# Hybrid encoder layer: where the embedding's products wait for their store, and the order of work in the state-space part

## The chip, the cores and the metric

The kernel runs on one core of one Trainium2 chip, in one launch. The metric is device time in microseconds. Of the kernel before, three runs took 2042.01 to 2043.56 us, median 2043.38 us. The profile is of one more execution.

## The reference, cut to what matters

One encoder layer on x (1024 tokens of width 1024, f32): a half-step feed-forward, one projection into attention and state-space inputs, attention and state-space side by side, an out-projection of both halves, a second half-step feed-forward, and an embedding gated into the result. Four layer norms stand between these.

```python
x = LN0(alpha*x + 0.5*SwiGLU_1(x))
u = x @ W_in                     # q | k | v | z | x_ssd | B | C | dt_fwd | dt_bwd
a = attention(q, k, v)           # 512 wide
s = ssd(x_ssd, B, C, dt)         # 512 wide: forward scan + backward scan + D * x, gated by SiLU(z)
x = LN1(alpha*x + concat(a, s) @ W_out)
x = LN2(alpha*x + 0.5*SwiGLU_2(x))
x = LN3(alpha*x + sigmoid(x @ W_g + b_g) * (p @ W_p))
```

The scan works on 8 chunks of 128 tokens; for one direction and one chunk it is

```python
y_diag = (C B^T * L) @ (x*dt)    # inside the chunk
y_off  = (C @ state) * decay     # what comes from the chunks before
state  = state * chunk_decay + B^T @ (x * dt * decay_to_end)
```

and the skip term adds `D * x`, one factor per head of 64 columns. Two places are touched by the change: `p @ W_p`, which does not depend on x and is computed at the very start, and the state-space scan with the out-projection around it.

## The kernel before, in words

Matrix products are made exact enough by splitting every f32 operand into a rounded high part and the rest (`split`, `split_into`, L79 to L87: ScalarE casts the high part, VectorE subtracts it for the low part), so a product of one 128-row step is three TensorE matmuls (`mm3`, L109). A block of weights that is split waits in the ring (tiles `blk`), what is not yet split in tiles `raw`. In parts of the program `in_order` fixes the order of an engine's instructions as the code is written; elsewhere a scheduler that plans ahead orders VectorE, ScalarE, GpSimd and the DMA queue of SyncE (SP's queue). TensorE's order is as the code is written throughout.

**The start** (`begin`, L561). While x is still being loaded, TensorE computes the embedding's product: 16 units (`ple_unit`, L577), each 128 tokens by 512 columns, 6 matmuls. A unit's result is copied out of PSUM into a small buffer (tiles `u2`, `u3`, `p5`, `p1`) by ScalarE, or for units 1, 3, 5 and 7 by VectorE, and stored in DRAM (`eD`); the store is issued by ScalarE (L590), behind its next copy. Between the units the list `beside` says which splits of x (`put`), differences (`less`) and splits of the first weights (`left`) are written there; TensorE, VectorE and ScalarE keep this order. x and the first weights come in by SP's queue. Two of the weights' blocks (`g0`, `u0`) are loaded into ring tiles behind the units. The products of the first feed-forward begin behind unit 15, so the third one of them (`p1`, L695) and all that follows waits for the 16 units.

**State space, right to left** (`ssd_right`, L1211). For the chunks 7 down to 0, three steps overlap: `front` (TensorE makes the decay exponents, ScalarE takes Exp of two 128x1024 tiles, and copies `cb`), `mid` (`y = D * x` by eight 128x64 ScalarE activations in `scale_heads`, then VectorE forms the weights `W`), `offdiag` with `next_state` (16 ScalarE activations, 128x64, and VectorE's adds), and `back` (8 small matmuls, the sum into `y`, a store to `yd`). At loop steps 0, 1 and 8 a filler is written behind: `spilled`, the attention half of the out-projection for one token tile, 24 matmuls of 128x512. Before the loop, `weights(0)` (L1479) splits that half's four weight blocks of 1024 columns, each as two halves in a row.

**State space, left to right** (`ssd_left`, L1282). For the chunks 0 up to 7: `offdiag`, `next_state`, the product with the gate `zs`, the norm, and a filler (five `resident`, out-projections that stay in memory, then five `mixed`, the state-space half of the out-projection with its layer norm). Two chunks later `turn` transposes the result on TensorE. The last `resident` calls `weights(1)`, which loads four 1024-wide blocks through the two `raw` tiles and splits them; the first `mixed` is the first to use them. Loads of the out-projection's accumulators (`acc1`, L1486, L1522), of the norm's factors (`ln_g`, `ln_b`), of `y2` (L1298), `zs`, `xb`, `bc` and of weights share SP's queue.

Of the kernel before, what the change touches and what calls it, by code (L numbers as in the profile page):

```python
# [9 lines left out]
F32 = mybir.dt.float32  # L10
# [26 lines left out]
class Layer:  # L37
# [522 lines left out]
    def begin(self, pool, tmp, spare):  # L560


        nc, I = self.nc, self.I
        V, A = nc.vector, nc.scalar
        self.eD = self.dram.tile([NT, P, D], F32, name="eD")
        a = slice(0, 512)

        first = [pool.tile([P, 4, 512], F32, name=f"xET4{j}") for j in "hl"]
        first = [t[:, k] for t in first for k in range(4)]
        todo, kept = [], []  # L570

        def loaded(src):
            r, b = first.pop(0), self.ring.tile([P, 2, 512], F32R, name="blk")
            nc.sync.dma_start(out=r, in_=src)
            todo.append((b, r))
            return b

        def ple_unit(i, t, n):
            c = slice((t % 4) * P, (t % 4 + 1) * P)
            o = self.pss()  # L580
            self.mm3(o, [((pT[t // 4][k][:, 0, c], pT[t // 4][k][:, 1, c]), (we[n][k][:, 0], we[n][k][:, 1])) for k in range(2)])
            e = tmp.tile([P, 512], F32, name=("u2", "u3", "p5", "p1", "p1", "p1")[i % 6])
            kept.append((self.eD[t][:, n * 512:(n + 1) * 512], e))
            if i < 8 and i % 2:
                V.tensor_copy(e, o)
            else:
                A.copy(out=e, in_=o)
                while kept:
                    dst, src = kept.pop(0)
                    A.dma_start(out=dst, in_=src)  # L590

        pT, we = [[], []], [[], []]

        def load_p(h, k):
            pT[h].append(loaded(I["pT"][:, k, h * 512:(h + 1) * 512]))

        def load_e(n, k):
            we[n].append(loaded(I["we"][n][:, k * 512:(k + 1) * 512]))

        for k in range(2):  # L600
            load_p(0, k)
            load_e(0, k)
        for load in (load_e, load_p):
            for k in range(2):
                load(1, k)
        nc.sync.dma_start(out=self.ident, in_=I["ident"])
        raws = []
        for k in range(4):
            for src in (I["xT"][:, k], I["xT"][:, k + 4]):
                i = len(raws)  # L610
                if i < 7:
                    r = self.rp.tile([P, D], F32, name="raw") if i < 5 else spare.tile([P, D], F32, name=f"wr{i - 4}")
                    nc.sync.dma_start(out=r, in_=src)
                    raws.append((r[:, :512], r[:, 512:]))
                else:
                    raws.append([tmp.tile([P, 512], F32, name=n) for n in ("h1", "h2")])
                    for j, r in enumerate(raws[-1]):
                        nc.sync.dma_start(out=r, in_=src[:, j * 512:(j + 1) * 512])
        sg = [tmp.tile([P, S], F32, name="sg") for f in range(3)]
        for f in range(2):  # L620
            nc.sync.dma_start(out=sg[f], in_=I["wi1"][f, 0])
        (r11, r12), (r21, r22) = ([[r[j] for r in raws[i::2]] for j in range(2)] for i in range(2))
        s = [tmp.tile([P, 512], F32, name=f"s{k + 1}") for k in range(4)]

        for b, r in todo:
            self.split_into(b, r)
        X = dict(zip(("B11", "B21", "T1", "B22"), sum(self.new_xT(), [])))
        for n in ("T2", "T3", "T4"):
            X[n] = [pool.tile([P, 4, 512], F32R, name=f"xE{n}{j}") for j in "hl"]

        def put(name, k, src):
            return lambda: self.put(X, name, k, a, src)

        def less(out, x, y):
            return lambda: V.tensor_tensor(out=out, in0=x, in1=y, op=ALU.subtract)

        w = {}

        def left(f, i):
            def do():  # L640
                w[f, i] = self.split(sg[f][:, i * 512:(i + 1) * 512])
            return do

        def sum1(k):
            return [less(r11[k], r12[k], r11[k]), less(s[k], r22[k], r11[k])]

        def staggered(first, then):

            return first(0) + sum((first(k + 1) + then(k) for k in range(3)), []) + then(3)

        def b11(k):
            return [put("B11", k, r11[k])]

        def b21(k):
            return [put("B21", k, r21[k])]

        def t2(k):
            return [put("T2", k, s[k])]

        def sum4(k):  # L660
            return [less(r21[k], r21[k], s[k])]


        beside = [[], b11(0) + b21(0), b11(1), b21(1) + sum1(0), b11(2), b21(2) + sum1(1), b11(3), sum1(2), b21(3), [left(0, 0)] + sum1(3),
                  [left(0, 1)] + t2(0) + sum4(0), [left(1, 0)] + sum4(1), [left(1, 1)] + t2(1) + sum4(2), t2(2) + sum4(3), t2(3), []]
        units = [(t, n) for u in range(2) for n in range(2) for t in range(u * 4, u * 4 + 4)]
        for i, ((t, n), work) in enumerate(zip(units, beside)):
            ple_unit(i, t, n)
            for do in work:
                do()  # L670
        work = []

        g0 = self.ring_raw(I["wi1"][0, 0])
        u0 = self.ring_raw(I["wi1"][0, 1])
        nc.sync.dma_start(out=sg[2], in_=I["wi1"][2, 0])
        a11, a12, a21, a22 = g0[:, :512], g0[:, 512:], u0[:, :512], u0[:, 512:]
        m = [tmp.tile([P, 512], F32, name=f"s{k + 1}") for k in range(4)]
        blocks0 = []

        def block(src):  # L680
            return lambda: blocks0.append(self.split(src))

        work += [lambda: V.tensor_tensor(out=m[0], in0=a21, in1=a22, op=ALU.add), less(m[1], m[0], a11), block(m[1]), block(m[0])]
        work += [put("T1", k, r11[k]) for k in range(4)] + [left(2, 0), left(2, 1), less(m[2], a11, a21)]
        work += staggered(lambda k: [less(r12[k], r22[k], r12[k])], lambda k: [put("T3", k, r12[k])])
        work += [block(m[2]), less(m[3], a12, m[1])]
        work += [put("T4", k, r21[k]) for k in range(4)]
        work += [block(a22), block(m[3])]
        work += [put("B22", k, r22[k]) for k in range(4)]
        pre = []  # L690
        for f, n in enumerate((5, 6, 7)):
            p1 = tmp.tile([P, 512], F32, name="p1")
            p = [self.product(w[f, i], X[b]) for i, b in enumerate(("B11", "B21"))]
            for _ in range(n):
                work.pop(0)()  # L695
            A.copy(out=p1, in_=p[0])
            V.tensor_tensor(out=sg[f][:, :512], in0=p1, in1=p[1], op=ALU.add)
            pre.append((p1, sg[f]))
        for do in work:
            do()  # L700
        return X, pre, blocks0
# [513 lines left out]
    def ssd_right(self, c, loaded, fillers):  # L1215
# [33 lines left out]

        def mid(ch, xb, bc, E, cb):  # L1250
            y = two.tile([P, 512], F32, name="y", bufs=3)
            self.scale_heads(y, xb, dsk)
            V.tensor_tensor(out=E[1], in0=E[1], in1=E[0], op=ALU.add)
            W = E[1]
            for g in range(2):
                V.tensor_tensor(out=W[:, 4 * g:4 * g + 4], in0=W[:, 4 * g:4 * g + 4], in1=cb[:, g].unsqueeze(1).broadcast_to([P, 4, P]), op=ALU.mult)
            return W, y
# [10 lines left out]
        for i in range(NT + 2):  # L1268
# [3 lines left out]
            if 0 <= ch + 1 < NT:  # L1272
                c1 = ch + 1
                xb, bc, E, cb = F.pop(c1)
                B[c1] = (c1, xb, bc) + mid(c1, xb, bc, E, cb)
                if st is not None:
                    self.offdiag(two, st, 1, c1, bc, B[c1][4])
                if c1 > 0:
# [6 lines left out]
    def ssd_left(self, c, loaded, late, mixT, fillers):  # L1285
# [28 lines left out]
        for ch in range(NT):  # L1314
# [3 lines left out]
            zs, y = rest.pop(ch)  # L1318
            if st is not None:
                self.offdiag(two, st, 0, ch, bc, y)  # L1320
            if ch < NT - 1:
                st = self.next_state(two, st, 0, ch, xb)
            V.tensor_tensor(out=y, in0=y, in1=zs, op=ALU.mult)
# [8 lines left out]
                o = slice(g * 256, (g + 1) * 256)  # L1332
                V.scalar_tensor_tensor(out=y[:, o], in0=y[:, o], scalar=r[:, g:g + 1], in1=snorm[:, o], op0=ALU.mult, op1=ALU.mult)
            waiting.append((ch, y))
            fillers[ch]()
            if len(waiting) > 2:
                turn(*waiting.pop(0))
        for w, filler in zip(waiting, fillers[NT:]):
            filler()
            turn(*w)  # L1340

# [74 lines left out]
    def run(self):  # L1416
# [61 lines left out]

        def weights(half):  # L1479
            if half:  # L1480
                wm[1].extend(self.wload(I["wm"][4 + k]) for k in range(4))
            else:
                wm[0].extend([self.split(r[:, i * 512:(i + 1) * 512]) for i in range(2)] for r in early)

        def attention_half(t, a):
            nc.sync.dma_start(out=a, in_=y0[t])  # L1486
# [253 lines left out]
```

## Time and profile before

| what | us |
|---|---|
| three runs, median (lowest, highest) | 2043.38 (2042.01, 2043.56) |
| profiled execution | 2044.08 |
| its span, first to last instruction | 2042.3 |
| TensorE busy | 1988.6 (97%) |
| VectorE busy | 1529.7 (75%) |
| ScalarE busy | 877.2 (43%) |
| GpSimd busy | 471.9 (23%) |

The profiled execution is 0.70 us above the median of the runs, and 1.8 us of it lie outside the span. TensorE is idle for 53.7 us of the span in all. In the rows, PE is TensorE, DVE is VectorE, ACT is ScalarE, POOL is GpSimd; SPq and ACTq are the DMA queues that SyncE and ScalarE feed. A timeline's row has the start, the time from there to the end of the group, and in brackets the idle time before it and what ended that.

### The profile page before, as it was taken

How to read it: one execution, taken by the hardware profiler on the slowest of the kernel's cores; microseconds unless marked ns; L12 is line 12 of the kernel's file. 1: busy time of each engine (PE TensorE's matmuls, PEld its weight loads, DVE VectorE, ACT ScalarE, POOL GpSimd, SP SyncE). 2: the span in 40 equal slices, each digit the busy share in tenths (PEclk: the TensorE clock that was granted, in tenths of full speed). 3: DMA queues.
4: the chain of work that ended last, by engine and by line, in shares of the span. 5: the costliest groups of instructions: out<-in, count | busy, mean ns of one | idle time of the engine just before them, and what ended most of it. 6: DMA issues, size and time to landing. Idle time of an engine off the chain costs nothing.

```text
span 2042.3 us, 25910 instructions
## 1 busy us (share of the span) xinstructions
PE 1988.6 (97%) x9244; PEld 1630.9 (80%) x9244; DVE 1529.7 (75%) x2289; ACT 877.2 (43%) x1552; POOL 471.9 (23%) x342
## 2 busy tenths in 40 slices
PE   8999999999999999999999999899999999999998
PEld 6788888887888889777887777678888888888886
DVE  6977876866669658658998769887777777567698
ACT  5433333324444124537888874333333333443311
POOL 0444445430001132000001001164444541000011
PEclk9999999999999999999999999999999999999999
DMA  7433553549865201230003382133444546986122
GB/s 259 150 119 139 191 185 139 186 171 345 283 233 176 79 29 57 62 115 11 1 1 114 100 299 83 67 128 133 178 174 152 190 142 241 366 271 226 50 73 93
DMA packets 145513, 306.80 MB, mean 150 GB/s; under 512 B 17218, under 2 KB 29890, under 8 KB 145384
## 3 DMA queue, kind: packets, MB, share of 16 engines
q1 hardware_dynamic: 143080, 300.96, 42.0%
q10 hardware_dynamic: 2304, 4.20, 0.5%
q8 instruction: 72, 1.18, 0.2%
q14 instruction: 57, 0.47, 0.1%
HBM read 213.67 MB, written 91.42 MB: 149 GB/s over the span
## 4 chain that ended last, share of the span: by engine, by line
PE 85%; DVE 6%; DMA 3%; ACT 2%; issue 2%; POOL 1%; SPq 0%; ACTq 0%; DVEq 0%; POOLq 0%
PE sm L117 49%; PE sm L482 12%; PE big L482 9%; PE big L117 3%; PE big L1053 3%; PE sm L1075 3%; PE sm L1090 1%; PE sm L1091 1%; DVE blk L85 1%; PE big L205 1%; DMA wr<-in_wo_dram 1%; PE sm L1159 1%; PE sm L1170 0%; DMA wr<-in_xT_dram 0%; DVE xl L85 0%
## 5 line engine op out<-in xcount | busy, mean ns | idle before, releaser
L117 PE MATMUL sm<-xh,blk 128*128 128x512 f32 x1424 | 448.4, 395 | 0.0
L117 PEld LDWEIGHTS sm<-xh,blk 128*128 128x128 f32 x1424 | 268.4, 189 | 62.7 <-DVE blk L85 0.3
L117 PE MATMUL sm<-xl,blk 128*128 128x512 f32 x736 | 288.3, 395 | 0.0
L117 PE MATMUL sm<-blk,xl 128*128 128x512 f32 (+2 forms) x784 | 240.6, 374 | 0.0
L117 PE MATMUL sm<-blk,xh 128*128 128x512 f32 (+2 forms) x584 | 207.2, 385 | 5.3 <-DVE blk L85 4.9
L103 ACT CAST blk<-raw 128x512 fp32r<-128x512 f32 (+1 forms) x166 | 99.6, 610 | 230.9 <-PE sm L117 145.1
L85 DVE TENSOR_TENSOR blk<-raw,blk 128x512 fp32r<-128x512 f32 (+1 forms) x166 | 162.3, 987 | 36.2 <-ACT blk L103 34.8
L85 DVE TENSOR_TENSOR blk<-s,blk 128x512 fp32r<-128x512 f32 x176 | 150.4, 859 | 40.1 <-ACT blk L103 38.2
L103 ACT CAST blk<-s 128x512 fp32r<-128x512 f32 x176 | 108.1, 621 | 158.3 <-PE sm L117 134.2
L180 POOL TENSOR_TENSOR ln_k<-ln_k,mhalf 128x1 f32<-128x1 f32 x32 | 41.1, 1290 | 561.1 <-DVE ln_k L179 544.1
L117 PEld LDWEIGHTS sm<-xl,blk 128*128 128x128 f32 x736 | 138.7, 189 | 32.7 <-DVE u L365 0.3
L117 PEld LDWEIGHTS sm<-blk,xl 128*128 128x128 f32 x784 | 143.3, 188 | 26.1 <-issue 0.7
L482 PE MATMUL sm<-xh 128*128 128x512 f32 x576 | 139.7, 391 | 1.9 <-DVE u L365 1.9
L85 DVE TENSOR_TENSOR xh<-blk,xh 128x1024 fp32r<-128x1024 f32 x78 | 96.8, 1241 | 57.0 <-ACT xh L430 50.9
L246 POOL TENSOR_TENSOR s<-raw 128x512 f32<-128x512 f32 x41 | 63.3, 1545 | 328.0 <-DVE blk L85 287.6
L117 PEld LDWEIGHTS sm<-blk,xh 128*128 128x128 f32 x584 | 110.3, 189 | 28.4 <-DVE blk L85 6.7
L85 DVE TENSOR_TENSOR xl<-blk,xl 128x1024 fp32r<-128x1024 f32 x76 | 92.8, 1220 | 49.6 <-ACT xl L430 45.0
L430 ACT CAST xl<-blk 128x1024 fp32r<-128x1024 f32 x76 | 79.8, 1050 | 115.2 <-PE big L482 39.8
L482 PEld LDWEIGHTS sm<-xh 128*128 128x128 f32 x576 | 107.7, 188 | 24.9 <-DVE u L365 2.3
L430 ACT CAST xh<-blk 128x1024 fp32r<-128x1024 f32 x78 | 81.9, 1050 | 103.7 <-PE sm L482 42.0
L482 PE MATMUL sm<-xl 128*128 128x512 f32 x480 | 117.0, 393 | 0.0
L117 PE MATMUL sm<-xET2h,blk 128*128 128x512 f32 x352 | 111.3, 397 | 1.2 <-DVE blk L85 1.2
(313 smaller groups left out, 4100.9 us busy)
## 6 DMA issues: line engine op xcount, KB each, us to landing
raw<-in_wi_dram SPq DMA_DIRECT2D x84, 512.0 KB
blk<-hS SPq DMA_DIRECT2D x154, 256.0 KB
hS<-h SPq DMA_DIRECT2D x88, 256.0 KB
wr<-in_wo_dram SPq DMA_DIRECT2D x44, 512.0 KB
blk<-wT SPq DMA_DIRECT2D x88, 256.0 KB
hS<-sg SPq DMA_DIRECT2D x66, 256.0 KB
wT<-wr SPq DMA_DIRECT2D x66, 256.0 KB
blk<-in_wo_dram SPq DMA_DIRECT2D x66, 256.0 KB
```

What stands on the lines that cost most here:

```text
L85: (eng or self.nc.vector).tensor_tensor(out=out, in0=full, in1=hi.bitcast(F32), op=ALU.subtract)
L103: self.nc.scalar.copy(out=b[:, 0, :n], in_=src)
L117: self.nc.tensor.matmul(ps, lhsT=a, rhs=b, start=(i == 0), stop=(i == n - 1))
L180: nc.gpsimd.tensor_tensor(out=r, in0=v, in1=self.mhalf[:, :1], op=ALU.pow)
L205: nc.tensor.transpose(out=ps[:, k], in_=a[:, k * P:(k + 1) * P], identity=self.ident)
L246: G.tensor_tensor(out=s1, in0=a21, in1=a22, op=ALU.add)
L430: A.copy(out=b[:, :, 0], in_=r)
L482: nc.tensor.matmul(ps[q], lhsT=b[:, 0, x, cut], rhs=b[:, 1, y], start=j == i == 0, stop=j == NP - 1 and i == 2)
L1053: nc.tensor.matmul(ps[:, n * 512:(n + 1) * 512], lhsT=Q[:, h, q0:q0 + P], rhs=K[:, h // 4, j, n * 512:(n + 1) * 512], start=j == 0, stop=j ...
L1075: nc.tensor.transpose(out=pt[:, k], in_=pr[:, kk * P:(kk + 1) * P], identity=self.ident)
L1090: nc.tensor.matmul(po, lhsT=vw, rhs=pth[:, k], start=k == 0, stop=False)
L1091: nc.tensor.matmul(po, lhsT=vw, rhs=ptl[:, k], start=False, stop=k == KD - 1)
```

## The change

At the start, all 16 units are copied out by ScalarE, four to a tile, into four tiles whose memory later holds blocks of x that are needed late (`xh10`, `xl10`, `xl11`, and `xET3h`); the 16 stores are issued on SP's queue, behind the loads of x and of the first weights. `g0` and `u0` become one tile `gu` in the memory of `xh11`, loaded ahead of the third `sg`. The splits in `beside` are spread anew: the `left` splits stand beside units 12 and 13 instead of 9 to 12. In the state-space part `y = D * x` becomes one VectorE multiplication per chunk; `weights(0)` and `weights(1)` split all first halves ahead of the second halves, and `weights(1)` loads 512-wide pieces. The filler of step 8 in `ssd_right` and the first one in `ssd_left` are written earlier: ahead of the last `offdiag` of the one and ahead of the first `next_state` of the other.

```diff
@@ begin
-            e = tmp.tile([P, 512], F32, name=("u2", "u3", "p5", "p1", "p1", "p1")[i % 6])
-            kept.append((self.eD[t][:, n * 512:(n + 1) * 512], e))
-            if i < 8 and i % 2:
-                V.tensor_copy(e, o)
-            else:
-                A.copy(out=e, in_=o)
-                while kept:
-                    dst, src = kept.pop(0)
-                    A.dma_start(out=dst, in_=src)
+            e = kept[i // 4][:, i % 4]
+            A.copy(out=e, in_=o)
+            with self.behind(mybir.EngineType.SP):
+                nc.sync.dma_start(out=self.eD[t][:, n * 512:(n + 1) * 512], in_=e)
...
-        for f in range(2):
-            nc.sync.dma_start(out=sg[f], in_=I["wi1"][f, 0])
+        gu = self.xp.tile([P, 4, 512], F32, name="xh11").rearrange("p (a b) c -> p a (b c)", b=2)
+        for dst, f, j in ((sg[0], 0, 0), (sg[1], 1, 0), (gu[:, 0], 0, 0), (gu[:, 1], 0, 1), (sg[2], 2, 0)):
+            nc.sync.dma_start(out=dst, in_=I["wi1"][f, j])
...
-        beside = [[], b11(0) + b21(0), b11(1), b21(1) + sum1(0), b11(2), b21(2) + sum1(1), b11(3), sum1(2), b21(3), [left(0, 0)] + sum1(3),
-                  [left(0, 1)] + t2(0) + sum4(0), [left(1, 0)] + sum4(1), [left(1, 1)] + t2(1) + sum4(2), t2(2) + sum4(3), t2(3), []]
+        beside = [[], b11(0) + b21(0), [], b11(1) + b21(1) + sum1(0), [], b11(2) + b21(2) + sum1(1), b11(3) + b21(3) + sum1(2), sum1(3),
+                  t2(0) + sum4(0), t2(1) + sum4(1), t2(2) + sum4(2), t2(3) + sum4(3), [left(0, 0), left(0, 1)], [left(1, 0), left(1, 1)], [], []]
...
-        g0 = self.ring_raw(I["wi1"][0, 0])
-        u0 = self.ring_raw(I["wi1"][0, 1])
-        nc.sync.dma_start(out=sg[2], in_=I["wi1"][2, 0])
-        a11, a12, a21, a22 = g0[:, :512], g0[:, 512:], u0[:, :512], u0[:, 512:]
+        X["T1"], X["T3"], X["T4"] = self.unit(1, 0), rest("T3"), rest("T4")
+
+        a11, a12, a21, a22 = (gu[:, i, j * 512:(j + 1) * 512] for i in range(2) for j in range(2))
@@ ssd_right
-            self.scale_heads(y, xb, dsk)
+            V.tensor_tensor(out=self.heads(y), in0=self.heads(xb[:, :512]), in1=self.per_head(dsk), op=ALU.mult)
...
                 B[c1] = (c1, xb, bc) + mid(c1, xb, bc, E, cb)
+                if c1 == 0:
+                    fillers.pop(i)()
                 if st is not None:
                     self.offdiag(two, st, 1, c1, bc, B[c1][4])
@@ ssd_left
                 self.offdiag(two, st, 0, ch, bc, y)
+            if ch == 0:
+                fillers.pop(0)()
             if ch < NT - 1:
                 st = self.next_state(two, st, 0, ch, xb)
...
-            fillers[ch]()
+            if ch:
+                fillers.pop(0)()
@@ weights
-                wm[1].extend(self.wload(I["wm"][4 + k]) for k in range(4))
+                blocks = []
+                for i in range(2):
+                    for k in (4, 6):
+                        r = self.rp.tile([P, 1024], F32, name="raw")
+                        halves = [r[:, j * 512:(j + 1) * 512] for j in range(2)]
+                        for j, h in enumerate(halves):
+                            nc.sync.dma_start(out=h, in_=I["wm"][k + j, :, i * 512:(i + 1) * 512])
+                        blocks += [self.split(h) for h in halves]
             else:
-                wm[0].extend([self.split(r[:, i * 512:(i + 1) * 512]) for i in range(2)] for r in early)
+                blocks = [self.split(r[:, i * 512:(i + 1) * 512]) for i in range(2) for r in early]
+            wm[half].extend(zip(blocks[:4], blocks[4:]))
```

The order of instructions moves at three places that matter. ScalarE at the start, behind the splits of p and of the embedding's weights; `raw` and `xh00`, `xh01` are x before and after the split, `sm` is PSUM. Before:

```order
L587 COPY u2_211<-sm_204 128x512
L590 DMA eD_127<-u2_211 128x512
L224 CAST xh00_190<-raw_147 128x512
L224 CAST xh01_192<-raw_149 128x512
L587 COPY p5_234<-sm_227 128x512
L590 DMA eD_127<-u3_221 128x512
L590 DMA eD_127<-p5_234 128x512
L224 CAST xh00_190<-raw_151 128x512
L224 CAST xh01_192<-raw_153 128x512
L587 COPY p1_260<-sm_253 128x512
L590 DMA eD_127<-p1_247 128x512
```

With the change:

```order
L585 COPY xh10_130<-sm_204 128x512
L585 COPY xh10_130<-sm_213 128x512
L224 CAST xh00_198<-raw_151 128x512
L224 CAST xh01_200<-raw_153 128x512
L585 COPY xh10_130<-sm_226 128x512
L585 COPY xh10_130<-sm_235 128x512
L224 CAST xh00_198<-raw_155 128x512
L224 CAST xh01_200<-raw_157 128x512
L585 COPY xl10_131<-sm_250 128x512
L585 COPY xl10_131<-sm_259 128x512
L224 CAST xh00_198<-raw_159 128x512
```

Units 0 to 5 now all end in a copy on ScalarE, where those of units 1, 3 and 5 were VectorE's, and the stores are gone from between its copies and casts.

SP's queue at the turn from the right part to the left part; `acc1` are accumulators of the out-projection, `y2` the chunks' sums that the left part goes on with. Before:

```order
L1486 DMA acc1_10327<-y0_86 128x1024
L1486 DMA acc1_10405<-y0_86 128x1024
L149 DMA ln_g_10280<-in_ln_g_dram 128x1024
L150 DMA ln_b_10281<-in_ln_b_dram 128x1024
L1298 DMA y2_10289<-yd_9562 128x512
L1298 DMA y2_10293<-yd_9562 128x512
L1298 DMA y2_10357<-yd_9562 128x512
L1298 DMA y2_10435<-yd_9562 128x512
L1486 DMA acc1_10483<-y0_86 128x1024
L1136 DMA xb_10520<-xbn_6914 128x768
```

With the change:

```order
L1507 DMA acc1_10228<-y0_86 128x1024
L1507 DMA acc1_10336<-y0_86 128x1024
L1507 DMA acc1_10414<-y0_86 128x1024
L1271 DMA yd_9549<-y_10134 128x512
L1507 DMA acc1_10503<-y0_86 128x1024
L1507 DMA acc1_10592<-y0_86 128x1024
L1543 DMA acc1_10717<-y1_9547 128x1024
L1543 DMA acc1_10819<-y1_9547 128x1024
L1543 DMA acc1_10891<-y1_9547 128x1024
L149 DMA ln_g_10211<-in_ln_g_dram 128x1024
L150 DMA ln_b_10212<-in_ln_b_dram 128x1024
L1307 DMA y2_10220<-yd_9549 128x512
```

Two accumulator loads of 512 KB stood ahead of the norm's factors and of the first `y2`; now eight do.

VectorE in the left part, around the norm of chunk 0 (`y2_10289` before, `y2_10220` with the change; `yss`, `rs_t` and `yr` are the norm's small tiles). Before, where `acc1_10405` is the second filler's accumulator:

```order
L1348 SCALAR_TENSOR_TENSOR acc1_10405<-sm_10407,acc1_10405 128x512
L1328 TENSOR_SCALAR yss_10312<-yss_10312 128x2
L124 TENSOR_TENSOR rs_t_10320<-yr_10318 128x2
L125 TENSOR_TENSOR rs_t_10320<-rs_t_10320,yss_10312 128x2
L126 TENSOR_SCALAR rs_t_10320<-rs_t_10320 128x2
L127 TENSOR_TENSOR yr_10318<-yr_10318,rs_t_10320 128x2
L1333 SCALAR_TENSOR_TENSOR y2_10289<-y2_10289,yr_10318,snorm_10287 128x256 x2
L1348 SCALAR_TENSOR_TENSOR acc1_10405<-sm_10421,acc1_10405 128x512
```

With the change, where `acc1_10414` is the third filler's:

```order
L1339 TENSOR_SCALAR yss_10273<-yss_10273 128x2
L1339 TENSOR_SCALAR yss_10321<-yss_10321 128x2
L1360 SCALAR_TENSOR_TENSOR acc1_10414<-sm_10430,acc1_10414 128x512
L124 TENSOR_TENSOR rs_t_10281<-yr_10279 128x2
L124 TENSOR_TENSOR rs_t_10329<-yr_10327 128x2
L125 TENSOR_TENSOR rs_t_10281<-rs_t_10281,yss_10273 128x2
L125 TENSOR_TENSOR rs_t_10329<-rs_t_10329,yss_10321 128x2
L126 TENSOR_SCALAR rs_t_10281<-rs_t_10281 128x2
L126 TENSOR_SCALAR rs_t_10329<-rs_t_10329 128x2
L127 TENSOR_TENSOR yr_10279<-yr_10279,rs_t_10281 128x2
L127 TENSOR_TENSOR yr_10327<-yr_10327,rs_t_10329 128x2
L1344 SCALAR_TENSOR_TENSOR y2_10220<-y2_10220,yr_10279,snorm_10218 128x256 x2
```

The last step of chunk 0's norm, on which its transposes wait, stood ahead of the second filler's last add, and now stands behind the third filler's.

## Rows read from the trace of the kernel before

**Rows 1.** The page, part 1: busy us, share of the span, instructions.

```profile
PE 1988.6 (97%) x9244; PEld 1630.9 (80%) x9244; DVE 1529.7 (75%) x2289; ACT 877.2 (43%) x1552; POOL 471.9 (23%) x342
```

**Rows 2.** Timeline of PE, first 45 us: start, us, instructions, idle before.

```profile
6.95 12.36 PE L117 MATMUL sm<-blk 128*128 128x512 f32 x42 [6.95 <-DVE blk L85]
22.33 14.16 PE L117 MATMUL sm<-blk 128*128 128x512 f32 x54 [3.02 <-DVE p L585]
36.33 0.40 PE L117 MATMUL sm<-xl,blk 128*128 128x512 f32 x1
...
37.02 0.39 PE L117 MATMUL sm<-xl,blk 128*128 128x512 f32 x1
```

**Rows 3.** Stretches: busy us (instructions) by engine, PEclk, DMA share, GB/s.

```profile
10.00:20.00 10.00, 9.31 (x36) 7.20 (x35) 3.37 (x5) 2.78 (x6) 0.00 (x0) 1.00 1.03 412
24.00:26.00 2.00, 2.00 (x6) 1.61 (x5) 2.00 (x5) 0.78 (x2) 0.00 (x0) 0.50 1.03 404
90.00:400.00 310.00, 309.94 (x1333) 250.75 (x1332) 233.50 (x293) 100.11 (x160) 145.56 (x97) 1.00 0.45 161
```

**Rows 4.** Timeline of ACT, 12 to 24 us.

```profile
18.61 0.33 ACTq L590 DMA_DIRECT2D eD<-u  x1
...
20.33 1.14 ACT L224 CAST xh<-raw 128x512 fp32r<-128x512 f32 x2 [5.35 <-DMA wr<-in_xT_dram]
```

**Rows 5.** Timeline of DVE, 12 to 32 us.

```profile
14.01 1.29 DVE L85 TENSOR_TENSOR xl<-raw,xh 128x512 fp32r<-128x512 f32 x2 [0.78 <-ACT xh L224]
```

**Rows 6.** Timeline of PE, 66 to 72 us.

```profile
68.75 0.73 PE L117 MATMUL sm<-xET2h,blk 128*128 128x512 f32 x2 [1.16 <-DVE blk L85]
```

**Rows 7.** What PE waited for, 1100 to 1178 us: us, times, longest.

```profile
PE sm L1159 <- DVE state L1176: 2.8, 4, 1.7
PE sm L117 <- DVE blk L85: 2.2, 3, 1.4
PE sm L1170 <- ACT xs L1153: 1.7, 2, 1.2
```

**Rows 8.** Stretches of the state-space part, columns as in rows 3.

```profile
1131.00:1163.00 32.00, 28.91 (x179) 22.55 (x178) 24.52 (x34) 32.00 (x113) 0.00 (x0) 1.00 0.37 111
1176.00:1178.00 2.00, 1.98 (x5) 1.14 (x6) 0.00 (x0) 2.00 (x9) 0.00 (x0) 0.58 0.50 178
1177.00:1199.00 22.00, 22.00 (x90) 17.94 (x91) 12.97 (x30) 16.15 (x66) 1.40 (x2) 0.94 0.98 370
...
1262.00:1280.00 18.00, 15.44 (x82) 12.61 (x83) 17.93 (x36) 12.09 (x28) 1.46 (x1) 1.00 0.22 89
```

**Rows 9.** Timeline of PE, 1100 to 1181 us: four chunks and the end.

```profile
1129.51 1.90 PE L1262 MATMUL sm<-xb,Eb 128*128 128x64 f32 x16
...
1135.14 1.89 PE L1262 MATMUL sm<-xb,Eb 128*128 128x64 f32 x16
...
1161.89 1.89 PE L1262 MATMUL sm<-xb,Eb 128*128 128x64 f32 x16
...
1176.02 2.17 PE L1170 MATMUL sm<-xs,xb 128*128 128x256 f32 x4 [1.20 <-ACT xs L1153]
1177.63 0.99 PE L117 MATMUL sm<-blk,xh 128*128 128x512 f32 x1
```

**Rows 10.** Timeline of SP's queue, 1170 to 1222 us.

```profile
1176.46 0.82 SPq L1486 DMA_DIRECT2D acc<-y  x2
...
1178.60 2.66 SPq L1298 DMA_DIRECT2D y<-yd  x4
```

**Rows 11.** Timeline of DVE, 1177 to 1200 us.

```profile
1186.72 0.69 DVE L1323 TENSOR_TENSOR y<-y,zs 128x512 f32<-128x512 f32 x1 [0.59 <-DMA y<-yd]
...
1191.61 0.88 DVE L1333 SCALAR_TENSOR_TENSOR y<-y,yr,snorm 128x256 f32<-128x256 f32 x2
```

**Rows 12.** What PE waited for, 1199 to 1346 us.

```profile
PE sm L117 <- DVE blk L85: 2.8, 1, 2.8
```

More of the change, by code (lines that the diff above doesn't have):

```diff
@@ L569, in begin @@
         first = [t[:, k] for t in first for k in range(4)]
-        todo, kept = [], []
+        todo = []
+        kept = [where.tile([P, 4, 512], F32, name=name) for where, name in ((self.xp, "xh10"), (self.xp, "xl10"), (pool, "xET3h"), (self.xp, "xl11"))]
         def loaded(src):
@@ L626, in begin, with rest @@
             self.split_into(b, r)
-        X = dict(zip(("B11", "B21", "T1", "B22"), sum(self.new_xT(), [])))
-        for n in ("T2", "T3", "T4"):
-            X[n] = [pool.tile([P, 4, 512], F32R, name=f"xE{n}{j}") for j in "hl"]
+        X = dict(B11=self.unit(0, 0), B21=self.unit(0, 1))
+        def rest(n):
+            return [pool.tile([P, 4, 512], F32R, name=f"xE{n}{j}") for j in "hl"]
+        X["T2"] = rest("T2")
         def put(name, k, src):
@@ L688, in begin, with b22, do @@
         work += [block(a22), block(m[3])]
-        work += [put("B22", k, r22[k]) for k in range(4)]
+        X["B22"] = None
+        def b22(k):
+            def do():
+                X["B22"] = X["B22"] or self.unit(1, 1)
+                self.put(X, "B22", k, a, r22[k])
+            return do
+        work += [b22(k) for k in range(4)]
         pre = []
@@ L1334, in ssd_left @@
             waiting.append((ch, y))
-            fillers[ch]()
+            if ch:
+                fillers.pop(0)()
             if len(waiting) > 2:
                 turn(*waiting.pop(0))
-        for w, filler in zip(waiting, fillers[NT:]):
+        for w, filler in zip(waiting, fillers):
             filler()
```

## The prediction

> **What bounds the kernel now.** I read the page's first part, then the timeline of TensorE, then the lists of what it waited for, and last the other engines' timelines where it waited. TensorE is busy for 1988.6 of 2042.3 us [rows 1]: the time is its work plus 53.7 us of idle time and of slow clock. Only what takes a TensorE wait away, or adds one, counts, and between the start and the state-space part such a shift passes on whole, since TensorE hardly waits there: 309.94 busy of 310 us [rows 3]. The diff touches two regions: the first 95 us, and 1097 to 1346 us (state space and out-projection).
>
> At the start TensorE gets its first split operands at 6.95 us, runs 42 of the 96 small products, waits 3.02 us for a VectorE copy, runs the other 54 and reaches the first feed-forward product at 36.33 us [rows 2]. Three matmuls take 0.70 us (36.33 to 37.02), 0.233 each, so the 54 should take 12.6 us; they took 14.0. The rest is the clock: the granted clock was 0.50 of the higher level, 2.4 GHz, in 24 to 26 us, after the wait [rows 3]. ScalarE is the cause of the wait: it had its store of `u` to issue and could not until 18.61, then `p` at 19.96, and between its copy and its casts of x at 20.33 it was idle 5.35 us [rows 4]. The transfers run at their limit meanwhile (412 GB/s, share 1.03) [rows 3].
>
> In the state-space part's right loop ScalarE is the bound: 32.00 of 32 us, TensorE 28.91, VectorE 24.52 [rows 8]. TensorE waits there for `state`, `xs` and the splits of the weights [rows 7]. In the left part the loads are at the limit first (share 0.98, 370 GB/s), and from about 1216 us VectorE: 17.93 of 18 us in 1262 to 1280, where TensorE has 15.44 [rows 8].
>
> **Start.** Removed: 16 store issues on ScalarE (0.33 us each, and the waits before them) and 4 copies on VectorE; added: 4 copies on ScalarE and 16 issues on SP's queue. The stores now go into memory that is not reused by the next unit, so no unit waits for a store. A copy takes 0.6 us against 1.4 us of a unit's six matmuls. If nothing else waits, TensorE runs all 96 in a row: 19.31 + 54 x 0.233 = 31.9 in place of 36.33, **-4.4**. What must then be ready at 31.9 are the splits of x's `B11` and the first weights, `left(0, 0)`, which wait for x (its last parts land about 20 us) and for some 28 VectorE operations at a pitch of 0.60 us (two in 1.29, each 0.69 long) [rows 5]: from the first of them at 14.01 that is 30.8, just hidden. If it isn't, each VectorE operation too late costs 0.6. On SP's queue the 16 stores (4 MB, about 10 us at 412 GB/s) stand ahead of the next weights, so those land by about 40 us, before the third product needs them. Given back: at 68.75 TensorE waits 1.16 us for a `blk` split [rows 6]; all before it is earlier, and with the change two more VectorE operations stand ahead of that split: **+0.7**, taken between 0 and 1.4. The start: **-3.7**, between -5 and -1 (only the 1.4 of clock gained).
>
> A rule speaks against this: the Trainium skill, "DMA: Bandwidth & Descriptors", section "Issuing engines are not separate DMA queues", says that transfers end up on the same 16 engines whoever starts them, and that another issuer only saves the sequencer's time. By it the move would save ScalarE's 16 x 0.33 us alone, none of it on TensorE's path, and the start would be 0. Here the row at 18.61 shows an issue that waits, with copies and casts behind it, so I hold with the row; the rule's case is a rival below.
>
> **Right part.** (1) `weights(0)` with first halves first: the first product needs 4 splits in place of 7. The three waits are 2.2 us [rows 7]; with splits at the pace of VectorE about 0.3 stays: **-1.9**. (2) `y = D * x`: 8 of the 27 ScalarE operations of a chunk go; one VectorE operation comes, 0.69 by the nearest row of its size, `y<-y,zs` [rows 11], taken between 0.6 and 1.2. By [rows 8], 113 ScalarE operations in 32 us are 4.2 chunks of 7.6 us, and 34 VectorE operations in 24.5 us, seven to a chunk, 5.0 us in each. ScalarE falls to under 6 us in a chunk, VectorE rises to 5.7, both about TensorE's own 5.63 (1129.51 to 1135.14) [rows 9]. Four chunks took 1161.89 - 1135.14 = 26.75 where 4 x 5.63 is 22.52: **-4.2**, of which up to 2 may stay if VectorE's turn comes late. (3) The filler moved ahead of the last `offdiag` covers the last `xs`: the wait of 1.20 goes, and with it the slow stretch behind it (granted clock 0.58 and 0.57 in four us, the first matmuls of 1176.02 and 1177.63 twice as long) [rows 8, 9], 1.7: **-2.9**. Sum **-9.0**: the first filler of the left part starts at about 1168.6, not 1177.63.
>
> **Left part.** (4) That filler now stands ahead of `next_state(0)`, so `offdiag(1)` follows `next_state(0)` with nothing between, and TensorE waits for the state's copy, 0.69 and the signals: **+0.9**. (5) SP's queue: 8 accumulators and 2 rows of factors, 5 MB, stand ahead of the first `y2`, where 2 MB did. Before, the four `y2` were issued from 1178.60 and the first was used at 1186.72 with 0.59 us of wait [rows 10, 11]. 3 MB more at 370 GB/s are 8.1 us; `y2` is there about 15 us behind the first filler's start, and the norm ends 5 to 6 us behind that (1186.72 to 1192.5 before). The transposes of chunk 0 come behind the third filler, about 22 us from the start: 5.6 (filler) + 0.9 + 0.9 + 1.7 + 5.6 + 1.7 + 5.6. So the load alone is just hidden, but VectorE now has the third filler's last add ahead of that norm's end: it can't go on before TensorE has ended the filler, and then takes 0.7 + 8 x 0.17 + 0.9 us and signals. TensorE waits 2.4 to 4.5 us where it didn't: **+3.7**. (6) `weights(1)` in halves: the wait of 2.8 us for its splits [rows 12] mostly goes, but VectorE is near its bound behind it, so I count half: **-1.4**, between 0 and -2.8. Left part **+3.2**, between 0 and +7.
>
> Sum: -3.7 - 9.0 + 3.2 = -9.5. The profiled execution of 2044.08 would be 2034.6; it stands 0.70 above the median of the runs, so about **2034 us**.
>
> **Rivals.** *The start gains nothing* (the rule above, as a mechanism of this kernel): the start is set by x's landing and by VectorE's 28 operations, and TensorE only waits at 31.9 instead of at 19.3. For it: transfers at their limit, VectorE 2.00 of 2 us in 24 to 26 [rows 3]. Against: VectorE loses four copies, and had only 3.37 of 10 us in 10 to 20, while ScalarE's casts came late. Then 2043.4 - 5.8 = 2037.6.
> *The left part takes the right part's gain back*: VectorE is the bound from 1216 to 1300, and its work there isn't less, so TensorE arrives 9 us earlier only to wait there. For it: 17.93 of 18 us. Against: before that stretch VectorE has 9 idle us in 1177 to 1199 (12.97 of 22) [rows 8], so its work can start earlier too. Right and left -1, start -1 to 0: 2041.5 to 2043, no change that can be told; 0.2%, 4.1 us, is about what a measurement of this kernel can tell.
> *Slower*: the eight accumulators hold SP's queue so long that `y2`, `xb` and the weights, all behind them, come late in turn. One accumulator is 512 KB, 1.4 us at 370 GB/s. It decides once the first `y2` lands later than 19 us behind the first filler, against my 15: then TensorE waits for each `turn` and `offdiag` of the left part, about 8 x 1.7 = 14 us beside the +3.2, and the gain of 12.7 becomes +4.5: 2048. For it: share 0.98 already. Against: the same bytes moved before, only in another order, and the loads start 9 us earlier.
>
> **How the numbers follow.** The forecast has 0.58, with its own range 2028 to 2038.5. The start without gain 0.18 (0.14 of it beyond 0.2%), the gain given back 0.17 (0.05 beyond), slower 0.07. So faster by over 0.2% has 0.77, within 0.2% 0.16, slower 0.07. The range for 8 in 10 goes from 2028 (start -5, right -9.7, left 0, the sum -14.7) to 2041, where the lower end of the given-back case lies.
>
> **What would show it.** Right: no TensorE gap between 19 and 23 us, the first feed-forward product near 32; in the right loop TensorE busy over 31 of 32 us and ScalarE below 30; the left part's first filler near 1165 (start included); a new wait of 2 to 5 us for `y2` or of about 0.9 us for `state` in the left part. Wrong: a wait for `blk`, `xl` or `raw` at 30 to 36 us; in the right loop a wait for `y`, `W` or `toff` on VectorE in place of `state`; more than two waits for `y2` in the left part; or the stretch 1216 to 1346 longer by what the right part gained.

## The result and the profile after

The changed kernel took 2026.26 us (median of 4 runs, 2023.06 to 2027.48), the kernel before beside it 2042.70: a ratio of 0.9921, interval 0.9903 to 0.9939. The forecast of 2034, range 2028 to 2041, had the direction; the time lies below the range. A second measurement, told below, gave 0.9931 (0.9919 to 0.9944), 2026.40 against 2040.42 from 21 runs of before.

The two profiled executions, cut where TensorE begins the same instruction in both:

| stretch | before | after | difference |
|---|---|---|---|
| start, to the first feed-forward product | 36.33 | 30.94 | -5.39 |
| from there to the right part (the change touches its first 60 us alone) | 1069.91 | 1064.56 | -5.35 |
| right part, to the left part's first filler | 71.39 | 61.33 | -10.06 |
| left part and out-projection | 131.23 | 132.83 | +1.60 |
| second feed-forward and the end | 733.44 | 733.74 | +0.30 |

0.87 us of the right part's 10.06 is `next_state(0)`, which now stands behind that filler: moved, not saved. So the right part gained 9.2, and the left part lost 0.7.

TensorE at the start of the changed kernel (start, us, instructions, idle before), to be held against [rows 2]; then its wait that answers to [rows 6]:

```profile
6.69 24.42 PE L117 MATMUL sm<-blk 128*128 128x512 f32 x96 [6.69 <-DVE blk L85]
30.94 0.40 PE L117 MATMUL sm<-xl,blk 128*128 128x512 f32 x1
...
63.88 0.73 PE L117 MATMUL sm<-xET2h,blk 128*128 128x512 f32 x2 [1.75 <-DVE blk L85]
```

The 96 products run in one piece. The wait at 64 us is 0.6 longer than before, but most of that is regained in the next 30 us: the twelfth product on `xET4l` starts 63.62 us behind the first feed-forward product, and in the kernel before 63.45. ScalarE in the same stretch, for [rows 4]: no store stands between copies and casts, and its idle times are those for TensorE's next result.

```profile
12.07 0.59 ACT L585 COPY xh<-sm 128x512 f32<-128x512 f32 x1 [0.94 <-PE sm L117]
12.55 1.14 ACT L224 CAST xh<-raw 128x512 fp32r<-128x512 f32 x2
13.60 0.59 ACT L585 COPY xh<-sm 128x512 f32<-128x512 f32 x1
14.82 0.59 ACT L585 COPY xh<-sm 128x512 f32<-128x512 f32 x1 [0.64 <-PE sm L117]
```

TensorE in the state-space part, for [rows 7, 9]: one wait at the entry, four chunks of 5.63 us, then the left part's new waits.

```profile
1100.81 0.50 PE L117 MATMUL sm<-blk,xh 128*128 128x512 f32 x1 [0.73 <-DVE blk L85]
...
1116.94 1.89 PE L1269 MATMUL sm<-xb,Eb 128*128 128x64 f32 x16
...
1139.46 1.90 PE L1269 MATMUL sm<-xb,Eb 128*128 128x64 f32 x16
...
1156.83 0.48 PE L117 MATMUL sm<-blk,xh 128*128 128x512 f32 x1
...
1164.31 1.13 PE L1166 MATMUL sm<-state,bc 128*128 128x256 f32 x4 [0.78 <-DVE state L1180]
...
1181.27 0.74 PE L1315 MATMUL sm<-ident,y 128*128 128x128 f32 x4 [2.06 <-DVE y L1344]
...
1228.38 0.83 PE L1315 MATMUL sm<-ident,y 128*128 128x128 f32 x4 [1.25 <-DVE y L1344]
```

Stretches of the changed kernel, columns as in rows 3, for [rows 8]. In the four chunks of the right loop all three engines are nearly full (first line), with TensorE setting the pace: ScalarE has 22.27 us of work in 22.52, 5.57 a chunk. Its 24.98 of 32 in the second line comes from the loop's end, where it has less to do. The clock falls behind the wait for `y2`; from 1196 to 1278 us VectorE is nearly full, 79.71 of 82 us.

```profile
1116.94:1139.46 22.52, 22.41 (x143) 18.29 (x144) 21.19 (x32) 22.27 (x74) 0.00 (x0) 1.00 0.51 154
1120.00:1152.00 32.00, 31.89 (x195) 26.45 (x196) 29.11 (x43) 24.98 (x76) 0.00 (x0) 1.00 0.37 116
1182.00:1184.00 2.00, 2.00 (x8) 1.59 (x7) 2.00 (x4) 0.58 (x1) 0.00 (x0) 0.58 0.95 335
1196.00:1207.00 11.00, 11.00 (x54) 9.11 (x53) 10.86 (x24) 8.60 (x30) 0.70 (x1) 1.00 0.70 229
1230.00:1243.00 13.00, 13.00 (x71) 10.97 (x70) 13.00 (x30) 6.59 (x17) 1.36 (x2) 1.00 0.30 121
1243.00:1261.00 18.00, 15.24 (x80) 12.15 (x78) 17.82 (x37) 12.70 (x28) 1.41 (x2) 1.00 0.15 59
```

### The profile page after: what moved, and what is told of

Same layout as the page of the kernel before. It is cut to its first block, busy times and chain, and to the rows that moved or that the text cites. A ratio compares the mean times of both kernels' runs of the same rounds, so it can differ in the third digit from the quotient of the medians.

```text
span 2023.4 us, 25860 instructions
## 1 busy us (share of the span) xinstructions
PE 1981.7 (98%) x9240; PEld 1628.7 (80%) x9244; DVE 1526.5 (75%) x2293; ACT 864.1 (43%) x1492; POOL 471.1 (23%) x342
## 4 chain that ended last, share of the span: by engine, by line
PE 89%; DVE 6%; issue 2%; DMA 1%; ACT 1%; POOL 1%; SPq 0%; DVEq 0%; POOLq 0%; ACTq 0%
PE sm L117 52%; PE sm L482 12%; PE big L482 9%; PE big L117 3%; PE big L1060 3%; PE sm L1082 3%; PE sm L1097 1%; PE sm L1098 1%; DVE blk L85 1%; PE big L205 1%; PE sm L1269 1%; PE sm L1177 1%; PE sm L1166 1%; DVE acc L191 0%; DMA raw<-in_wi_dram 0%
## 5 line engine op out<-in xcount | busy, mean ns | idle before, releaser
L85 DVE TENSOR_TENSOR blk<-s,blk 128x512 fp32r<-128x512 f32 x176 | 148.9, 851 | 37.9 <-ACT blk L103 36.1
```

Source lines behind the costliest of these rows:

```text
L85: (eng or self.nc.vector).tensor_tensor(out=out, in0=full, in1=hi.bitcast(F32), op=ALU.subtract)
```

## The experiments

Ratios are to the kernel before on the same chip, with their intervals. "Start" is the time of the first feed-forward product, "state space" the time from the right part's first decay exponents to the second feed-forward's first product (before: 36.33 and 202.6 us; changed: 30.94 and 194.2), both from each run's profile, which is one execution.

**The two halves of the change.** `start_only` is before with the hunks of `begin`, `scan_only` with all others.

> The kernel before with the change of the start alone (copies on ScalarE into late memory, stores on SP's queue, work beside the units spread anew); the state-space part is as before. The trace of the changed kernel gave 5.4 us in the start and 5.35 us in code that the change doesn't touch (3.3 at 468 to 502 us, 2.2 at 912 to 936 us). Theory 1: those 5.35 are differences between executions, so only the start counts: first feed-forward product near 31 us, 2037.5 us, and in the trace the wait at the L482 products near 470 may be there or not. Theory 2: they follow from the start: 2032 to 2034 us, and the trace has no TensorE wait over 0.5 us and no clock below 0.9 at 460 to 480 us.

> The kernel before with the state-space part's change alone; the start is as before. Theory 1: the difference of the two traces in that part holds: -10.1 in the right part, +1.6 in the left part, so -8.5: 2034 us; the first feed-forward product stays near 36.3 us. Rival: part of the 10.1 was only there because the part was entered with other DMA traffic or another clock: 2037 or more. If theory 2 of the run with the start alone holds, the wait near 472 us and the slow clock behind it are there as before.

`start_only` came to 0.9962 (0.9948 to 0.9976), start 30.36, state space 201.3; `scan_only` to 0.9962 (0.9949 to 0.9974), start 36.11, state space 195.2. The two add up to the whole, 0.9924. The median of `start_only`, 2032.71, lies where theory 2 had it, but both theories counted from the 2043 of the first runs; from the 2040.25 measured beside it, the 5.4 us of theory 1 are a ratio of 0.9974, within the interval. So the time alone does not decide. The stretch between the start and the state-space part does. It took 1069.9 in the profile of before, but 1064.8 with `scan_only`, whose start is that of before. Of all the kernels below, those with the old start took 1064.0 to 1067.8, those with the change's start 1064.6 to 1067.9. So its 5.35 us are a difference between executions (theory 1), and the profiled execution of before is a long one there. What varies is seen at the first down-projection products: TensorE in before, TensorE and then the stretch behind the wait in `y2_first` (told below), TensorE in the changed kernel:

```profile
472.01 1.98 PE L482 MATMUL sm<-xh 128*128 128x512 f32 x6 [1.88 <-DVE u L365]
```

```profile
466.56 1.65 PE L482 MATMUL sm<-xh 128*128 128x512 f32 x6 [1.97 <-DVE u L365]
```

```profile
468.00:472.00 4.00, 4.00 (x12) 3.10 (x12) 4.00 (x6) 1.31 (x2) 0.00 (x0) 0.57 0.98 348
```

```profile
465.12 1.66 PE L482 MATMUL sm<-xh 128*128 128x512 f32 x6 [0.24 <-DVE u L365]
```

The wait for `u` is 1.9 us long in the first two, with the clock near its lower level behind it, and this place takes 3.3 us more there than in the third, where it is 0.24. The long one comes with either start; over all fourteen profiles it lies between 0.24 and 1.97.

**What in the start did it.** `act_stores` is the changed kernel with the stores back on ScalarE, `dve_copies` with four copies back on VectorE, `small_tiles` with the small buffers back:

```diff
-            with self.behind(mybir.EngineType.SP):
-                nc.sync.dma_start(out=self.eD[t][:, n * 512:(n + 1) * 512], in_=e)
+            A.dma_start(out=self.eD[t][:, n * 512:(n + 1) * 512], in_=e)      # act_stores
...
-            A.copy(out=e, in_=o)
+            V.tensor_copy(e, o) if i < 8 and i % 2 else A.copy(out=e, in_=o)  # dve_copies
...
-            e = kept[i // 4][:, i % 4]
+            e = tmp.tile([P, 512], F32, name=("u2", "u3", "p5", "p1", "p1", "p1")[i % 6])  # small_tiles
```

> The changed kernel with the 16 stores of the embedding's products issued by ScalarE, each right behind its copy, in place of SP's queue; the memory that they are stored from is that of the change. My theory: what cost time was a store that had to wait, with copies and casts behind it on ScalarE; with ScalarE as issuer each issue takes 0.33 us and waits for the DMA eight before it, so part of the gap comes back: first product at 33 to 36 us, 2 to 5 us slower than the change (2028 to 2031). Rival, the memory alone did it (no reuse, so no wait): the first product stays at 31 to 32 us and the time within 1 us of the change's 2026.

> The changed kernel with the results of units 1, 3, 5 and 7 copied by VectorE as before, still into late memory and stored from SP's queue. My theory: the copy on VectorE, in order behind subtractions that wait for x, was where TensorE's 3.02 us wait ended; it comes back in part, first product at 33 to 35 us, 2 to 4 us slower than the change. Rival, the stores' issue on ScalarE alone was the cause: first product at 31 us, the same time as the change.

> The changed kernel with the 16 copies made into the small buffers of before (reused within the start), while the stores stay on SP's queue behind the loads. Theory: memory and queue belong together: the seventh copy waits for the first store, which stands behind 6.5 MB of loads until about 28 us, so the first feed-forward product comes at 42 us or later, 11 us or more slower than the change. Rival: the queue alone did it and the stores land in time: first product at 31 to 33 us.

`act_stores`: 0.9972 (0.9961 to 0.9983), start 37.33, more than my bounds: all of the start's gain is gone. `dve_copies`: 0.9942 (0.9929 to 0.9956), start 30.82: VectorE's copies cost the start nothing, my theory falls. `small_tiles`: one run, 2036.53; start 38.38, where I expected 42 or later. Memory and queue are both needed. ScalarE in `act_stores`, then in `small_tiles`:

```profile
13.27 0.59 ACT L585 COPY xh<-sm 128x512 f32<-128x512 f32 x1 [2.08 <-DMA raw<-in_xT_dram]
18.50 0.33 ACTq L586 DMA_DIRECT2D eD<-xh  x1
18.87 1.14 ACT L224 CAST xh<-raw 128x512 fp32r<-128x512 f32 x2 [5.01 <-DMA wr<-in_xT_dram]
```

```profile
27.70 0.59 ACT L585 COPY u<-sm 128x512 f32<-128x512 f32 x1 [8.31 <-DMA eD<-u]
```

The copy at 13.27 is done by 13.9, yet its store goes out at 18.50, when a load of x has landed: the issue waits for an earlier transfer of another queue, with casts and copies behind it. This wait is one of the program. In the trace the DMAs of both queues count their landing on eight semaphores in turn, and each issue first waits for the DMA eight before it, which had the same one. ScalarE has an instruction for that ahead of every store:

```profile
L586 ACTq EVENT_SEMAPHORE  x16: 17/17/17, 12.8 to 40.7; - x16
```

The store of 18.50 counts on the semaphore that the load of `wr` issued at 9.37 had last; in the kernel before it is the same for the store at 18.61 [rows 4]. So the rival of a start that gains nothing falls. By the rule of the Trainium skill behind it ("DMA: Bandwidth & Descriptors", section "Issuing engines are not separate DMA queues") another issuer saves only the time to issue. Here the first product comes 6.4 us later with ScalarE as issuer, and what holds ScalarE up is not the issue, 0.33 us, but the wait ahead of it, 5.01 us. Stores on ScalarE with semaphores of their own were not run. In the row of `small_tiles` the copy waits for the store of its buffer, which stands behind the loads.

**The parts of the state-space change.** Before with one part each (the hunks of the front's diff): `y_only`, `fillers_only`, `weights_only`.

> The kernel before with D * x on VectorE alone. Theory: in the right loop the four waits for state (2.8 us) and the wait for xs inside the loop (0.5) go, chunks take 5.63 us each, and ScalarE's xs at the end comes earlier, so that the wait of 1.20 us before the last next_state goes too: 4 to 7 us, 2034 to 2036. Rival: VectorE is now late in the loop, so waits for state stay and half or less is gained.

> The kernel before with the two fillers moved alone. Theory: the wait of 1.20 us for xs and the slow clock behind it go (2.9 us), the right loop keeps its waits for state, and the left part gets its new waits of 0.8 for state and 2 us for y2 with a slow clock behind: 0 to 1.5 us less than the kernel before. Rival: the wait for xs only moves, since ScalarE is behind in the loop: slower by 1 to 3 us.

> The kernel before with the order of the out-projection's weight splits alone. Theory: 1.8 us less at the entry of the right part (its waits of 2.2 us fall to about 0.7), and the wait of 2.8 us before the state-space half's first product goes, but VectorE, the bound behind it, takes that back: 1.8 us less in all. Rival: both stay, 4 us less.

`y_only` 0.9981 (0.9971 to 0.9991), state space 201.1, less than the 4 to 7 us expected: the waits for `state` are gone, that for `xs` (1.20) is not; 4.6 us are gained up to the first transposes and 3.1 given back behind them (its profiled execution is the longest of its ten). `fillers_only` 0.9990 (0.9981 to 1.0000), 201.3, close to what was expected, with new waits of 0.78 and 2.33 us. `weights_only` 1.0008 (0.9994 to 1.0021), 207.8: a miss. Its entry gains 1.8 us, and then TensorE waits the longer for ScalarE, which stays the bound, and runs near the lower clock behind that. (The profiled execution, 2046.38, is one of three among ten that took 2046 to 2049; the median is 2040.78, so 207.8 is more than usual, and what the usual execution does with the 1.8 us was not seen.) Its right loop and the stretch after:

```profile
1117.00:1161.00 44.00, 37.91 (x224) 28.44 (x222) 32.23 (x45) 44.00 (x152) 0.00 (x0) 1.00 0.33 106
1160.00:1172.00 12.00, 10.78 (x35) 9.25 (x36) 4.32 (x7) 2.00 (x9) 0.00 (x0) 0.57 0.19 66
```

Alone the three come to 0.9979, together to 0.9962. With the intervals of the three taken together (0.9960 to 0.9998) that difference is not shown. What the traces show is that the earlier entry is lost where ScalarE holds the loop back, and that the wait for `xs` of 1.20 goes with a filler in its place and stays without one.

**The left part.** `y2_first` is the changed kernel with the loads of six accumulators behind those of `y2`; `both` also cuts the first filler in two; `gate_pool` is `both` with the gate's product on GpSimd:

```diff
-            nc.sync.dma_start(out=a, in_=y0[t])
+            if t < 5:
+                nc.sync.dma_start(out=a, in_=y0[t])
+            else:
+                with self.tc.issue_after(self.y2_load):       # the y1 loads of mixed likewise
+                    nc.sync.dma_start(out=a, in_=y0[t])
...
-            fillers = [lambda t=t: resident(t) for t in range(3, NT)] + [lambda t=t: mixed(t) for t in range(3)]
+            fillers = [lambda n=n: half3(n) for n in range(2)] + [lambda t=t: resident(t) for t in range(4, NT)] + [lambda t=t: mixed(t) for t in range(3)]  # both; half3(n): half n of tile 3's filler
...
-            V.tensor_tensor(out=y, in0=y, in1=zs, op=ALU.mult)
+            nc.gpsimd.tensor_tensor(out=y, in0=y, in1=zs, op=ALU.mult)   # gate_pool
```

> The changed kernel with the accumulators of tiles 5 to 7 and 0 to 2 loaded behind the y2 loads, alone. Theory: the wait of 2.06 us for y2 at the first transposes and the slow clock behind it go, the 0.78 us for state stays: 3.7 us less than the change. Rival: the loads are late anyway, the wait for y2 stays above 1.5 us; or it turns into a wait for an accumulator that is now late, at the third filler (near 1176 us).

> The changed kernel with two more edits in the left part: the accumulators of tiles 5 to 7 and 0 to 2 are loaded behind the y2 loads on SP's queue, and the first filler is cut in its two halves of 12 matmuls, one ahead of next_state(0), one behind it. Theory (the left part's new waits come from the queue's order and from the missing cover): the waits of 0.78 us for state and 2.06 us for y2 go, and with the second the slow clock behind it (0.58 and 0.57 in four us), 1.7 us: 4.5 us less than the change, ratio to the kernel before near 0.990, 2020 to 2023 us. Rival (VectorE bounds the part from about 1200 us on): TensorE only waits later, first transpose near 1177 us but the out-projection's end within 1 us of the change's, and the time is the change's.

> The kernel with both edits of the left part, and in addition the gate's product y2 * zs of the eight chunks (128x512) on GpSimd in place of VectorE. Theory (what those two edits freed was taken back because VectorE is the bound from 1196 to 1278 us, 80.7 of 82 us busy): 8 operations of 0.6 us less on VectorE give 3 to 5 us between the first transpose and the out-projection's end against the run of both edits; ratio to the kernel before near 0.992. Rival: a GpSimd operation of this size takes about 1.3 us, lies in the chain of each chunk's norm, and the transposes wait for it: no gain.

`y2_first` 0.9946 (0.9931 to 0.9961), state space 194.6; `both` 0.9947 (0.9935 to 0.9960), 195.3: no gain in either, as the rival of `both` had it. TensorE in `both`:

```profile
1183.87 0.50 PE L117 MATMUL sm<-blk,xh 128*128 128x512 f32 x1 [1.01 <-DVE acc L1360]
...
1235.36 0.83 PE L1316 MATMUL sm<-ident,y 128*128 128x128 f32 x4 [1.82 <-DVE y L1345]
...
1265.96 1.12 PE L232 MATMUL big<-ident,xt 128*128 128x128 f32 x4 [4.68 <-DVE xt L1609]
...
1288.82 0.66 PE L232 MATMUL big<-ident,xt 128*128 128x128 f32 x4 [3.11 <-DVE xt L1609]
```

The first transposes wait no more, and TensorE is 3.3 us earlier there; but it waits longer for VectorE behind (4.68 where the change has 1.74 and 2.29), and the end is no earlier. `gate_pool`: 0.9923 (0.9910 to 0.9937), median 2024.76, state space 191.3, 4.1 less than `both` though each product takes 1.27 us or more on GpSimd: that fits VectorE's work as the bound (the expectation's 80.7 of 82 us is 79.71 in the trace of the change). Against the changed kernel's 2026.40, measured beside it, the gain is 1.6 us, and the intervals overlap: the best median, not shown to be faster than the change.

One rival stands. The scheduler orders VectorE anew in every kernel, and the second `xt`, for which TensorE waits 4.68 us in `both`, comes behind six splits of the next feed-forward's weights (`blk`) there, behind four in the changed kernel and behind one in `gate_pool`. VectorE in `both`, then in `gate_pool`:

```profile
1263.42 1.28 DVE L85 TENSOR_TENSOR blk<-sg,blk 128x512 fp32r<-128x512 f32 x2
...
1265.22 0.68 DVE L1609 TENSOR_TENSOR xt<-acc,acc 128x512 f32<-128x512 f32 x1
```

```profile
1257.98 0.69 DVE L85 TENSOR_TENSOR blk<-blk 128x512 fp32r<-128x512 f32 x1
1258.58 0.69 DVE L1609 TENSOR_TENSOR xt<-acc,acc 128x512 f32<-128x512 f32 x1
```

Five splits at a pitch of 0.6 us are 3 us, most of what lies between the two kernels. Whether VectorE's work or this order takes the gain of `both` back was not separated.

**The size again.** 

> The changed kernel once more, beside the kernel before on one chip. Its first runs gave a ratio of 0.9921 (0.9903 to 0.9939) from four runs of each; the terms that the two traces show in code that the change touches (start -5.4 and +0.6, right part -10.1, left part +1.6) are -13.3 us, a ratio of 0.9935, and kernels that differ from the change by little gave 0.9942 to 0.9947. If those terms are the whole effect, the ratio is 0.993 to 0.995. Rival: the 5.35 us in code that the change doesn't touch belong to it: 0.991 or less.

0.9931 (0.9919 to 0.9944), start 31.64, state space 193.0: the touched code's terms are the whole effect, as far as the interval tells.

## Why the prediction was wrong

The mechanisms were there; the sizes were too small, and the base was high. From 2034 to 2026.3 there are 7.7 us:

- **The base, 3.0.** I set the change against the median of three runs, 2043.38. In 21 runs the kernel before had 2040.42 (2036.57 to 2043.49); the three were among its longer ones, and my range carried nothing for that. With forecast and range 3.0 us lower the time would lie inside the range. I also counted on 0.2%, 4.1 us, as a difference that can be told; three runs of a kernel whose runs spread over 7 us don't give that.
- **Start, -3.7 forecast, -5.7 found.** First product: five kernels with the old start have 36.1 to 38.1, mean 36.8; seven with the change's start (`dve_copies` among them) 30.4 to 31.6, mean 30.8: -5.9, where I had -4.4. Of this, 0.5 is the trace of before, which lies on the short side: the five have gaps of 2.45 to 3.94 us with 3.5 to 6.0 us at the slow clock behind them, the trace of before 3.02 and 3.8. The rest is my 31.9: I counted from the end of the 42nd product at 19.31, while in the changed kernel the 43rd starts at 18.70, and the 54 take 12.24 us in place of 12.6. Given back: the wait at 64 us grew by 0.6 (forecast 0.7), but 0.2 is left of it by 100 us. The cause was right in the stores' issue on ScalarE; the copies on VectorE, taken away with it, had no share.
- **Right part, -9.0 forecast, -9.2 found.** Entry 1.8 (1.9); four chunks 1139.46 - 1116.94 = 22.52 (22.52 forecast); the rest is the filler over `xs`. Right, and VectorE was no bound, at 5.30 us in a chunk (5.7 forecast) beside TensorE's 5.63. ScalarE's 7.6 us in a chunk of before came of counting 27 operations to a chunk; ScalarE is full in the four chunks, so it is 26.75 / 4 = 6.7 us. It entered no term as a number.
- **Left part, +3.2 forecast, +0.7 found.** The wait for `state` came as worked out, 0.78 (0.9 forecast). That for `y2` was 2.06, under the 2.4 to 4.5 that I had; 1.7 of slow clock behind it, which I hadn't counted, bring it to the 3.7 forecast, by luck. The step that failed is to add the two to the time, with nothing given back behind them. TensorE then waits less for VectorE: the wait of 2.8 for `weights(1)` went whole where I counted half (in `start_only`, whose state-space part is that of before, it is 0.90, so part of it is the one trace), the layer norms' waits fell from 9.1 to 7.2 us, and one of 1.25 came. From 1196 to 1278 us VectorE is busy 79.71 of 82 us, and `both` takes the two waits away and ends no earlier. My second rival had the bound right and the consequence wrong: VectorE swallowed not the gain of the right part but most of the loss of the left. Whether through its work or through its planned order stays open, as said above.
- **The unchanged code, 0 forecast.** Two single traces put over 5 us there, and the experiments put none.

These terms, -5.7 - 9.2 + 0.7 = -14.2, agree with the second measurement's -14.0. The rivals of no gain in the start and of a slower kernel did not come: the accumulators' queue made one `y2` late, not eight.

## What to carry to other kernels

A DMA is issued in its engine's order, with the waits that the program puts ahead of it: a store on an engine that also casts and copies held these up for the landing of an unrelated load whose semaphore it shared. Put it on the queue of an engine that computes nothing, and give it memory that nobody waits for; either alone failed here. Before a new wait is added to a sum, ask which engine sets the pace of the stretch behind it: here a wait of TensorE was given back behind it, and so was what its removal had gained. The effects of edits to one loop need not add up: an earlier entry was lost where the loop's bound stood. And a median of three runs is too few for a base where 21 runs spread over 7 us.

## What the runs showed of the hardware

A wait of TensorE can cost nearly twice its length: behind that of 2.06 us at 1181 the granted clock of the changed kernel was 0.58 of the higher level, close to the lower, in 1182 to 1184; behind that of 1.97 at 468 in `y2_first` it was 0.57 in four us. It need not, and the length alone does not decide: behind one of 1.19 at the same place in `after_again` it stayed at 1.00, behind one of 1.78 in `act_stores` too, and behind 2.33 at the first transposes of `fillers_only`; behind 1.20 in the kernel before it was 0.58 [rows 8]. Executions of the kernel before lie up to 7 us apart, and stretches of identical code differed by over 5 us between profiles; 3.3 of these were such a wait with the slow clock behind it.
